# Last phase of a decoder-trunk kernel: T4 placed behind T3 and B22 for each pair, weights' parts pinned ahead of the norm's steps, three of w_out's sets stored as plain sums

## The chip, the cores and the metric

The kernel runs on one core of a Trainium2 chip. The metric is the device time of one execution in microseconds (us). Of the kernel before there are three timed runs and one profiled execution. TensorE is PE in the profile, VectorE DVE, ScalarE ACT, GpSimd POOL; SP is the engine whose queue issues most DMAs.

## The reference

One layer of a decoder trunk over 2048 positions of width 1024: adaLN modulation, a wide input projection, sliding-window attention and a pooled branch side by side, both projected and gated into y, then the part that this change is about:

```python
y = jax.nn.sigmoid(m_a) * a + jax.nn.sigmoid(m_p) * p
y = (y @ w_out[l]) * (1.0 + gate[:, None, :])
x = layer_norm(DEEPNORM_ALPHA * x + y, ln_gain[l], ln_bias[l])
```

All in float32. `layer_norm` works per position, over the 1024 columns.

## The kernel before, in words

**Products.** Every large matrix product is made of quads. A quad takes two blocks of 128 output rows and two column halves of 512, and computes its four results with seven half-size products instead of eight (Strassen-Winograd). The seven are named after the moving operand, a "set": B11, T1, T2, B21, T3, B22, T4. A set is 128x4x2x512 floats in SBUF: 4 slabs, each as a high part (the value rounded to fp32r) and a low part (the rest). The quad's own side, the "weights" W (here rows of y), is split in the same way just before use: ACT casts the high part (`CAST w_set<-W`), DVE subtracts to get the low part (`TENSOR_TENSOR w_set<-W,w_set`). A product is 12 matmuls of 128x512, three for each slab: high by high, high by low, low by high. So its first two matmuls need the cast alone.

A quad's split happens four times: **first** parts (for B11 and T1), **second** (T2, B21), **third** (T3, B22) and the half for T4. Between them POOL changes W in place: `sum1` (L294), `mid` (L298 and L299, of which L298 overwrites what the first parts are made from), `late` (L303).

**Groups and phases.** The last stage ("mix") has five phases; the fifth multiplies y by w_out. Each phase has groups of two quads, called x0 and x1 here. `ring` runs over the groups: `back` does T2 and B21 of x0 and of x1, then T3 and B22 of x0 and of x1, then T4 of x0 and of x1; `front` then opens the next group with B11 and T1 of each quad. After every product comes a `tick`, at which functions from `hooks` (set by group and position) and from the deferred list `due` are issued. In the last phase x0 holds rows 4g and 4g+1 of 128 positions, and x1 rows 4g+2 and 4g+3, for group g of 0 to 3.

**Norm.** `out_quad.consume` adds ALPHA times x to a result (L637, `wide<-wide,mm` or `wide<-wide,lg`). When both halves of a row are there, `norm_row` defers its steps by ticks: 1 sums (ACT over 128x1024), 2 mean and down (DVE, tiny) and squares (ACT), 3 rs (DVE, tiny), the power (POOL, 128x1) and (z-mean)*gain (DVE, 128x1024), 4 scale (DVE, 128x1024), 6 the store. Rows 13 to 15 use `last_norm` with BN_STATS on DVE and write the result in two halves.

**What sets the order.** Instructions issued through `act`, `dve`, `pool`, `sp` and `pe` (class `Ordered`) keep the program's order among themselves; those issued through `nc.scalar`, `nc.vector` and so on may be placed elsewhere by the scheduler that builds the program. Each engine then runs its instructions strictly as they stand. The splits by `pair_split` use `nc.scalar` and `nc.vector`, the norm's steps mostly the pinned ones.

**Sets of w_out.** They are made in the second phase of the kernel (stage "g1") by `sums_to`, split there by `kept_parts` (ACT cast, DVE low part, two stores) into `wo_d`, and loaded ready-made by `fill_set`, 1 MB a half set, by `PLAN`. Sets of other phases of "mix" are stored as plain sums, loaded as 512 KB a half into one of two `spare` tiles and split in place at `SPLIT_AT`. `planned` puts entries under 14 into the last group of the phase before, the others into the first group of the phase itself.

Of the kernel before, what the change touches and what calls it, by code (L numbers as in the profile page):

```python
# [19 lines left out]
P = 128  # L20
# [39 lines left out]
def kernel(  # L60
# [52 lines left out]
    def split_store(name):  # L113
        return {n: dp.tile([4, P, 2, CH], F32, name=f"{name}_{n}_split") for n in set_names}
# [3 lines left out]
    wo_d = split_store("wo")  # L118
# [157 lines left out]
    class Quad:  # L276
# [4 lines left out]
        def __init__(self, srcs, consume):  # L281
            self.srcs, self.consume = srcs, consume
# [69 lines left out]
    def front(ph, q, tick):  # L352
        w = pair_split(ph, q.first())
        q.mid()
        a, b = bank(), bank()
        product(a, w[0], "B11", True)
        tick()
        product(b, w[1], "T1", True)
        tick()
        return a, b, None, None  # L360

    def back(ph, grp, opened, nxt, own, tick, b22_first=False):
# [51 lines left out]
        if b22_first:  # L414
# [20 lines left out]
    def defer(ticks, f):  # L435
        due.append((now[0] + ticks, len(due), f))

    def run_due(every=False):
        while due and (every or any(d[0] <= now[0] for d in due)):
            d = min(due, key=lambda d: d[:2])  # L440
            due.remove(d)
            d[2]()

    def ring(ph, groups, opened, hooks, nxt, after, b22_first=False):
# [3 lines left out]
        def tick():  # L448
# [6 lines left out]
            run_due()  # L455

        for gi, grp in enumerate(groups):
            pos[:] = [gi, 0]
            own = gi % 2 == 0 and gi + 1 < len(groups)
            back(ph, grp, opened, (groups + [nxt])[gi + 1], own, tick, b22_first and gi == 0)  # L460
            if gi + 1 < len(groups):
                opened = [front(ph, q, tick) for q in groups[gi + 1]]
# [22 lines left out]
    def set_steps(ph, store):  # L485


        if store["B11"].shape[0] == 4:
            return [(p, lambda n=n, h=h: fill_set(n, h, store[n])) for p, n, h in PLAN]
        raw, todo = {}, []  # L490

        def fetch(k):
            name, half = PLAN[k][1:]
            raw[k] = ph.spare()
            sp.dma_start(raw[k], store[name][half].rearrange("p a b -> p (a b)"))

        def split(k):
            name, half = PLAN[k][1:]
            split_set(name, 2 * half, by_two(raw[k]), 2, (act, dve))

        for k, at in enumerate(SPLIT_AT):
            if k < 2:
                todo.append((0, lambda k=k: fetch(k)))
            todo.append((at, lambda k=k: split(k)))
            if k + 2 < len(SPLIT_AT):
                todo.append((at, lambda k=k: fetch(k + 2)))
# [78 lines left out]
    def norm_row(ph, row, z):  # L585
# [27 lines left out]
        for at, f in ((1, sums), (2, squares), (3, power), (4, scale), (6, store)):  # L613
            defer(at, f)

    def last_stats(row, n, zn):
        nc.vector.bn_stats(carry[:, row - 12, 6 * n : 6 * n + 6], zn)

    def last_norm(row, z):

        st, mv, rs = (carry[:, row - 12, a:b] for a, b in ((0, 12), (12, 14), (14, 15)))
        nc.vector.bn_aggr(mv, st)
        nc.vector.tensor_scalar(rs, mv[:, 1:2], EPS, None, ALU.add)
        nc.gpsimd.tensor_tensor(rs, rs, mhalf, ALU.pow)
        nc.vector.scalar_tensor_tensor(z, z, mv[:, 0:1], vec["gain"], ALU.subtract, ALU.mult)
        for n, q in enumerate((nc.sync, nc.scalar)):
            zn = cols(z, n)
            nc.vector.scalar_tensor_tensor(zn, zn, rs, cols(vec["lnb"], n), ALU.mult, ALU.add)  # L628
            q.dma_start(out[row * P : (row + 1) * P, n * CH : (n + 1) * CH], zn)

    def out_quad(k):
        def consume(ph, mi, n, src):
# [4 lines left out]
            nc.vector.scalar_tensor_tensor(zn, zn, ALPHA, src, ALU.mult, ALU.add)  # L637
            if row > 12:
                last_stats(row, n, zn)
            if n_done:  # L640
                if row > 12:
# [4 lines left out]
        return Quad(tuple(y_d[k + i].rearrange("p k q -> p (k q)") for i in range(2)), consume)  # L646
# [746 lines left out]
    with Pools("mix", spare=2, p=2, c=5) as ph:  # L1393
# [9 lines left out]
        for i, (groups, store) in enumerate(phases):  # L1403
# [7 lines left out]
            if i + 1 < len(phases):  # L1411
                planned(hooks, ph, phases[i + 1][1], True)
                nxt = phases[i + 1][0][0]
                after = lambda tick, nxt=nxt: [front(ph, q, tick) for q in nxt]
            else:
                for at, row in ((1, 2), (1, 3), (5, 4), (5, 5)):
# [66 lines left out]
```

## Time and profile before

| what | us |
|---|---|
| median of 3 timed runs | 1765.89 (1764.87 to 1765.94) |
| the profiled execution, its own time | 1766.12 |
| its span, first to last instruction | 1764.3 |
| PE busy in the span | 1702.9 |
| DVE, ACT, POOL busy | 1206.0, 931.8, 792.7 |
| mean granted TensorE clock | 0.992 |

The last phase begins at about 1593 us with the fronts of its first group (issued in the phase before), and its last matmul ends at about 1750. A timeline row reads: start, length (us), engine, line, operation, output<-input, shape, count, and in brackets the idle time of the engine just before and what ended it. A product of 12 matmuls takes 2.72 us from start to start. On PE `lg` and `mm` are accumulators; which product it is follows from the order T2, B21 (twice), T3, B22 (twice), T4 (twice, one row x24), then B11, T1 (twice).

### The profile page before, as it was taken

The numbers are of one execution on the slowest core, as the hardware profiler recorded it, in microseconds if no ns is written. First come the engines' busy times: TensorE is split into PE (matmuls) and PEld (weight loads), VectorE is DVE, ScalarE is ACT, GpSimd is POOL, SyncE is SP. The second block draws the span as 40 slices with busy tenths as digits, with TensorE's granted clock in tenths as the row PEclk, the third lists the DMA queues.
The fourth block names the chain that finished last, engine by engine and source line by source line (L and its number), as shares of the span: only waits on it lengthen the run. The fifth ranks groups of instructions, "written<-read, shape, count | busy, mean of one in ns | idle before, by whom it ended". The sixth has DMA issues, their size and how long they took to land. (4 is left out here: it accounts for less than half of the span.)

```text
span 1764.3 us, 24983 instructions
## 1 busy us (share of the span) xinstructions
PE 1702.9 (97%) x8248; PEld 1428.7 (81%) x8248; DVE 1206.0 (68%) x2180; ACT 931.8 (53%) x1969; POOL 792.7 (45%) x618
## 2 busy tenths in 40 slices
PE   6899999999999998999999999999999989999996
PEld 5688888888888887888788888888888768888785
DVE  5967665655777786766655367777867586765777
ACT  4544444545777775454444377777744333423451
POOL 2145454431356567434434125456762562364542
PEclk9999999999999999999999999999999999999998
DMA  9384767743354567687777634544796585689432
GB/s 365 112 279 179 270 210 273 271 148 132 108 173 146 172 219 294 245 281 254 246 274 262 231 98 132 175 155 149 258 356 225 182 257 182 226 314 384 166 143 99
DMA packets 180609, 381.30 MB, mean 216 GB/s; under 512 B 18800, under 2 KB 39296, under 8 KB 180480
## 3 DMA queue, kind: packets, MB, share of 16 engines
q1 hardware_dynamic: 173696, 363.66, 59.2%
q0 software_dynamic: 3552, 11.56, 1.7%
q10 hardware_dynamic: 3232, 4.49, 0.9%
q8 instruction: 65, 1.06, 0.2%
q14 instruction: 64, 0.52, 0.1%
HBM read 244.35 MB, written 138.44 MB: 217 GB/s over the span
## 5 line engine op out<-in xcount | busy, mean ns | idle before, releaser
L56 PE MATMUL mm<-set_B,w_set 128*128 128x512 f32 x3240 | 801.8, 396 | 17.5 <-DVE w_set L132 8.7
L56 PEld LDWEIGHTS mm<-set_B,w_set 128*128 128x128 f32 x3240 | 604.2, 189 | 147.4 <-DVE w_set L132 15.2
L56 PE MATMUL lg<-set_T,w_set 128*128 128x512 f32 x2088 | 505.9, 392 | 14.0 <-DVE w_set L132 8.6
L56 PEld LDWEIGHTS lg<-set_T,w_set 128*128 128x128 f32 x2088 | 390.8, 188 | 103.7 <-DVE w_set L132 14.0
L132 DVE TENSOR_TENSOR w_set<-W,w_set 128x1024 fp32r<-128x1024 f32 x162 | 224.1, 1383 | 175.7 <-ACT w_set L325 171.4
L325 ACT CAST w_set<-W 128x1024 fp32r<-128x1024 f32 x162 | 169.7, 1049 | 242.4 <-PE mm L56 195.6
L56 PE MATMUL mm<-set_T,w_set 128*128 128x512 f32 x1080 | 266.2, 394 | 0.0
L56 PEld LDWEIGHTS mm<-set_T,w_set 128*128 128x128 f32 x1080 | 201.1, 189 | 41.3
L294 POOL TENSOR_TENSOR W<-W,A 128x512 f32<-128x512 f32 x56 | 82.1, 1466 | 221.7 <-DMA W<-in_win_dram 55.9
L303 POOL TENSOR_TENSOR W<-W 128x512 f32<-128x512 f32 x56 | 80.1, 1431 | 155.5 <-DVE w_set L132 143.9
L56 DVE TENSOR_TENSOR o<-pv,o 64x128 f32<-64x128 f32 x256 | 72.4, 283 | 88.3 <-ACT o L56 85.4
L56 ACT ACTIVATE L<-L,nm 128x257 f32<-128x257 f32 (+1 forms) x256 | 127.2, 498 | 9.3 <-DVE nm L56 3.9
L298 POOL TENSOR_TENSOR W<-W 128x512 f32<-128x512 f32 x56 | 88.1, 1574 | 93.8 <-DVE w_set L132 84.7
L56 DVE CUSTOM_DVE_ANT_0 L<-lg,bt,nsink 128x256 f32<-128x256 f32 (+1 forms) x256 | 111.6, 473 | 5.0 <-PE lg L56 0.8
L299 POOL TENSOR_TENSOR W<-W 128x512 f32<-128x512 f32 x56 | 88.1, 1573 | 37.3 <-DMA W<-in_win_dram 28.1
L56 POOL TENSOR_TENSOR w_set<-W,w_set 128x1024 fp32r<-128x1024 f32 x14 | 33.7, 2405 | 139.6 <-ACT w_set L56 97.0
L56 POOL TENSOR_TENSOR p<-nxt,pg 128x512 f32<-128x512 f32 x32 | 42.0, 1311 | 106.4 <-DVE sm L56 102.8
L56 ACT COPY o<-pv 64x256 f32<-64x256 f32 x128 | 47.3, 370 | 78.1 <-PE pv L56 77.3
L56 DVE TENSOR_TENSOR ptl<-pt,pth 128x512 fp32r<-128x512 f32 (+1 forms) x128 | 85.7, 669 | 1.9 <-ACT pth L56 1.7
L56 DVE TENSOR_TENSOR k_lo<-spare,k_hi 128x512 fp32r<-128x512 f32 x61 | 63.2, 1041 | 28.8 <-ACT k_hi L56 15.0
L56 PE MATMUL lg<-kk,qs 128*128 128x256 f32 (+1 forms) x512 | 80.5, 279 | 0.0
L56 ACT ACTIVATE L<-L,sm 128x256 f32<-128x256 f32 (+1 forms) x128 | 64.3, 502 | 29.4 <-DVE sm L56 29.4
(208 smaller groups left out, 2304.9 us busy)
## 6 DMA issues: line engine op xcount, KB each, us to landing
W<-in_win_dram SPq DMA_DIRECT2D x48, 512.0 KB, 5.3
w_set<-wmix_d SPq DMA_DIRECT2D x32, 512.0 KB, 5.2
W<-in_win_dram SPq DMA_DIRECT2D x34, 256.0 KB, 3.4
A<-in_win_dram SPq DMA_DIRECT2D x34, 256.0 KB, 5.0
ag_d<-sig SPq DMA_DIRECT2D x32, 256.0 KB, 3.3
pg_d<-sig SPq DMA_DIRECT2D x32, 256.0 KB, 3.7
ma_d<-sig SPq DMA_DIRECT2D x32, 256.0 KB, 3.9
mp_d<-sig SPq DMA_DIRECT2D x32, 256.0 KB, 3.8
```

Of the source, the lines that this page charges most:

```text
L56: return lambda *args, **kw: self.tc.keep_in_program_order(op(*args, **kw))
L132: engine.tensor_tensor(dst, src, as32(hi), ALU.subtract)
L294: e.tensor_tensor(self.w[:, 1, :], self.w[:, 2, :], self.a22, ALU.add)
L298: e.tensor_tensor(x[:, 1, :], x[:, 1, :], x[:, 0, :], ALU.subtract)
L299: e.tensor_tensor(x[:, 2, :], x[:, 0, :], x[:, 2, :], ALU.subtract)
L303: e.tensor_tensor(x[:, 3, :], x[:, 3, :], x[:, 1, :], ALU.subtract)
L325: a.copy(by_two(hi), raw)
```

## The change

It has six parts.

1. `wo_d` keeps T3, B22 and T4 as plain sums (2x128x2x512) instead of split parts. `sums_to` stores each of them straight from the work buffer (`put`), with no cast and no subtraction; `set_steps` now decides for each set: split ones are filled as before, plain ones are fetched into a `spare` and split in place by ACT and DVE.
2. `out_quad` makes its quads `pinned`. In `back`, both T4 halves are split first; ahead of T4 of x1 the first parts of the next group's x0 are split through the pinned engines (`pinned_parts`), and in `front` those of x1 behind x0's B11.
3. The norm's steps are `soft`: the ticks behind T4 of x0 and behind x0's B11 leave them out, and `pinned_parts` issues those that are due behind its split.
4. The last group of the last phase runs pair by pair (`finish_rows`): T3, B22, T4 of x0, then B22, T3, T4 of x1.
5. Row 12 uses `last_norm` too; of rows 12 to 14 the final scale and stores are deferred by two ticks; these steps are pinned.
6. Rows 4 and 5 of x are loaded at position 9 of the first group, not 5.

```diff
-    wo_d = split_store("wo")
+    wo_d = {**split_store("wo", ("B11", "T1", "T2", "B21", "B12")), **{n: dp.tile([2, P, 2, CH], F32, name=f"wo_{n}") for n in ("T3", "B22", "T4")}}
...
-            if b12 or name != "B12":
+            if store[name].shape[0] == 2:
+                todo.append((at, lambda name=name, z=z: put(sp, store, name, i, x(*z))))
+            elif b12 or name != "B12":
...
-    def front(ph, q, tick):
-        w = pair_split(ph, q.first())
+    def front(ph, q, tick, ahead=None, follows=None):
+
+        w = ahead or pair_split(ph, q.first())
         q.mid()
         a, b = bank(), bank()
         product(a, w[0], "B11", True)
-        tick()
+        tick(not follows)
+        parts = pinned_parts(ph, follows)
         product(b, w[1], "T1", True)
         tick()
-        return a, b, None, None
+        return (a, b, None, None), parts
+
+    def pinned_parts(ph, q):
+        if q is None:
+            return None
+        w = pair_split(ph, q.first(), act, dve)
+        run_due()
+        return w
...
+        finish_rows = grp[0].pinned and not nxt
+        if finish_rows:
+            for x, (q, b, c, p5) in enumerate(st):
+                third(x)
+                w4 = half_split(ph, q.a22)
+                for f in (with_b22, with_t3) if x else (with_t3, with_b22):
+                    f(x)
+                product(c, w4, "T4")
+                tick()
+                q.consume(ph, 1, 0, c)
...
-        for q, b, c, p5 in st:
-            w = half_split(ph, q.a22)
+        ws = []
+        ahead = None
+        for x, (q, b, c, p5) in enumerate(st):
+            if q.pinned:
+                ws = ws or [half_split(ph, z[0].a22) for z in st]
+                w = ws[x]
+                if x:
+                    ahead = pinned_parts(ph, nxt[0])
+            else:
+                w = half_split(ph, q.a22)
             product(c, w, "T4")
-            tick()
+            tick(not q.pinned or x > 0)
             q.consume(ph, 1, 0, c)
+        return ahead
...
-    def run_due(every=False):
-        while due and (every or any(d[0] <= now[0] for d in due)):
-            d = min(due, key=lambda d: d[:2])
+    def run_due(every=False, soft=True):
+        while ready := [d for d in due if every or d[0] <= now[0] and (soft or not d[3])]:
+            d = min(ready, key=lambda d: d[:2])
...
+        for at, (kept_at, name, half) in zip(SPLIT_AT, PLAN):
+            if store[name].shape[0] == 4:
+                todo.append((kept_at, lambda n=name, h=half: fill_set(n, h, store[n])))
+                continue
+            todo.append((at, lambda n=name, h=half: split(n, h)))
+            fetch_at = ahead[-2] if len(ahead) > 1 else max(at - 4, 0)
+            todo.append((fetch_at, lambda n=name, h=half: fetch(n, h)))
+            ahead.append(at)
...
-            defer(at, f)
+            defer(at, f, True)
...
+        def scale():
+            for n, q in enumerate((sp, act)):
+                zn = cols(z, n)
+                dve.scalar_tensor_tensor(zn, zn, rs, cols(vec["lnb"], n), ALU.mult, ALU.add)
+                q.dma_start(out[row * P : (row + 1) * P, n * CH : (n + 1) * CH], zn)
+
+        if row < 15:
+            defer(2, scale)
+        else:
+            scale()
```

**Place 1, the passage from group 1 to group 2 of the last phase.** On DVE before (the tile after `wide` names a row: 15557 is row 4, 15771 row 6, 15559 row 5, 15825 row 7; `mean` marks (z-mean)*gain, `rs` in a `wide` row the scale, `lg` the result of T4; W_15844 belongs to x0 of the next group, W_15888 to x1):

```order
L56 SCALAR_TENSOR_TENSOR wide6_15557<-wide6_15557,mean_15867,wide0_15274 128x1024
L132 TENSOR_TENSOR w_set_15968<-W_15844,w_set_15967 128x1024
L637 SCALAR_TENSOR_TENSOR wide7_15559<-wide7_15559,lg_15751 128x512
L56 SCALAR_TENSOR_TENSOR wide6_15557<-wide6_15557,rs_15869,wide1_15276 128x1024
L56 TENSOR_SCALAR mean_15913<-total_15912 128x1
L56 TENSOR_SCALAR down_15914<-total_15912 128x1
L637 SCALAR_TENSOR_TENSOR wide3_15825<-wide3_15825,lg_15790 128x512
L132 TENSOR_TENSOR w_set_16017<-W_15888,w_set_16016 128x1024
```

On DVE now, at the same place (15610 is row 4, 15612 row 5, 15783 row 7; W_15802 is x0's, W_15846 x1's):

```order
L680 SCALAR_TENSOR_TENSOR wide7_15612<-wide7_15612,lg_15709 128x512
L56 TENSOR_TENSOR w_set_15899<-W_15802,w_set_15898 128x1024
L56 TENSOR_SCALAR rs_15827<-rs_15827 128x1
L56 SCALAR_TENSOR_TENSOR wide6_15610<-wide6_15610,mean_15825,wide0_15214 128x1024
L680 SCALAR_TENSOR_TENSOR wide3_15783<-wide3_15783,lg_15748 128x512
L56 SCALAR_TENSOR_TENSOR wide6_15610<-wide6_15610,rs_15827,wide1_15216 128x1024
L56 TENSOR_SCALAR mean_15871<-total_15870 128x1
L56 TENSOR_SCALAR down_15872<-total_15870 128x1
L56 TENSOR_TENSOR w_set_15946<-W_15846,w_set_15945 128x1024
```

The first parts of x0 moved ahead of row 4's step, but behind the result of x0's T4. On ACT before, at the same place (`total` marks sums, `down` squares):

```order
L56 ACTIVATE spare_15909,rs_15869<-wide6_15557,down_15868 128x1024
L325 CAST w_set_15967<-W_15844 128x1024
L56 ACTIVATE wide2_15771,total_15912<-wide2_15771 128x1024
L325 CAST w_set_16016<-W_15888 128x1024
L56 ACTIVATE spare_15959,rs_15915<-wide2_15771,down_15914 128x1024
L56 ACTIVATE wide7_15559,total_15937<-wide7_15559 128x1024
```

On ACT now:

```order
L56 ACTIVATE spare_15867,rs_15827<-wide6_15610,down_15826 128x1024
L56 CAST w_set_15898<-W_15802 128x1024
L56 ACTIVATE wide2_15729,total_15870<-wide2_15729 128x1024
L56 ACTIVATE spare_15921,rs_15873<-wide2_15729,down_15872 128x1024
L56 ACTIVATE wide7_15612,total_15894<-wide7_15612 128x1024
L56 CAST w_set_15945<-W_15846 128x1024
```

The cast of x1's first parts moved behind the squares of row 6 and the sums of row 5. The passages from group 0 to 1 and from 2 to 3 have the new order too.

**Place 2, the start of the last phase.** On DVE now (spare_15263 and spare_15290 hold the two halves of set T3; gp is a gate's tile of the phase before, multiplied into its result; W_15191 is x0's, W_15241 x1's):

```order
L56 TENSOR_TENSOR set_T3_13110<-spare_15263,set_T3_13110 128x2x512
L132 TENSOR_TENSOR w_set_15358<-W_15241,w_set_15357 128x1024
L605 TENSOR_TENSOR gp_15270<-mm_15068,gp_15270 128x512
L132 TENSOR_TENSOR w_set_15399<-W_15191,w_set_15398 128x1024
L56 TENSOR_TENSOR set_T3_13110<-spare_15290,set_T3_13110 128x2x512
L605 TENSOR_TENSOR gp_15294<-lg_15095,gp_15294 128x512
L132 TENSOR_TENSOR w_set_15446<-W_15241,w_set_15445 128x1024
L605 TENSOR_TENSOR gp_15315<-lg_15135,gp_15315 128x512
```

Before, the rows of set_T3 were not there, and each of the two `gp<-lg` stood one place earlier among the other six. On SP now, a little later (wo_B22 and wo_T4 are the plain sums):

```order
L56 DMA spare_15354<-wo_B22_96 128x1024
L56 DMA y_d_142<-wide5_14626 128x4x128
L56 DMA spare_15379<-wo_B22_96 128x1024
L56 DMA y_d_142<-wide7_14672 128x4x128
L290 DMA A22_15497<-y_d_142 128x512
L290 DMA A22_15539<-y_d_142 128x512
L56 DMA spare_15417<-wo_T4_97 128x1024
L289 DMA W_15496<-y_d_142 128x512
L56 DMA spare_15434<-wo_T4_97 128x1024
```

Four half sets of 512 KB stand where four of 1 MB were filled, and both A22 tiles of the next group now come ahead of T4's halves; before, they came behind them.

**Place 3, the end.** On DVE now, from the first half of row 15 on (16390 is row 15, 16337 row 14, 16111 row 13):

```order
L56 SCALAR_TENSOR_TENSOR wide_16390<-wide_16390,p_16356 128x512
L56 TENSOR_SCALAR carry<-carry 128x1
L56 SCALAR_TENSOR_TENSOR wide_16337<-wide_16337,carry,wide_15214 128x1024
L56 SCALAR_TENSOR_TENSOR wide_16111<-wide_16111,carry,wide_15216 128x512 x2
L56 BN_STATS carry<-wide_16390 128x6
L56 SCALAR_TENSOR_TENSOR wide_16337<-wide_16337,carry,wide_15216 128x512 x2
L56 SCALAR_TENSOR_TENSOR wide_16390<-wide_16390,lg 128x512
L56 BN_STATS carry<-wide_16390 128x6
```

Ahead of the last product's result (`lg`) stand the gain step of row 14 and the scales of rows 13 and 14; before, row 12's and row 13's steps stood there, and row 12 was stored last, in one piece of 512 KB.

More of the change, by code (lines that the diff above doesn't have):

```diff
@@ L459, in ring @@
             own = gi % 2 == 0 and gi + 1 < len(groups)
-            back(ph, grp, opened, (groups + [nxt])[gi + 1], own, tick, b22_first and gi == 0)
+            ahead = back(ph, grp, opened, (groups + [nxt])[gi + 1], own, tick, b22_first and gi == 0)
             if gi + 1 < len(groups):
-                opened = [front(ph, q, tick) for q in groups[gi + 1]]
+                pair = groups[gi + 1]
+                opened = []
+                for n, q in enumerate(pair):
+                    follows = pair[n + 1] if q.pinned and n + 1 < len(pair) else None
+                    o, ahead = front(ph, q, tick, ahead, follows)
+                    opened.append(o)
         result = after(tick) if after else None
@@ L485, in set_steps, with fetch, split @@
     def set_steps(ph, store):
-        if store["B11"].shape[0] == 4:
-            return [(p, lambda n=n, h=h: fill_set(n, h, store[n])) for p, n, h in PLAN]
         raw, todo = {}, []
[L492 to L506, printed above, removed]
+        def fetch(name, half):
+            raw[name, half] = ph.spare()
+            sp.dma_start(raw[name, half], store[name][half].rearrange("p a b -> p (a b)"))
+        def split(name, half):
+            split_set(name, 2 * half, by_two(raw[name, half]), 2, (act, dve))
+        ahead = []
+        for at, (kept_at, name, half) in zip(SPLIT_AT, PLAN):
[6 more added lines that the diff above has]
+            ahead.append(at)
         return todo
@@ L613, in norm_row @@
         for at, f in ((1, sums), (2, squares), (3, power), (4, scale), (6, store)):
[L614 removed]
+            defer(at, f, True)
     def last_stats(row, n, zn):
[L617 removed]
+        dve.bn_stats(carry[:, row - 12, 6 * n : 6 * n + 6], zn)
     def last_norm(row, z):
         st, mv, rs = (carry[:, row - 12, a:b] for a, b in ((0, 12), (12, 14), (14, 15)))
[L622 to L629, printed above, removed]
+        dve.bn_aggr(mv, st)
+        dve.tensor_scalar(rs, mv[:, 1:2], EPS, None, ALU.add)
+        pool.tensor_tensor(rs, rs, mhalf, ALU.pow)
+        dve.scalar_tensor_tensor(z, z, mv[:, 0:1], vec["gain"], ALU.subtract, ALU.mult)
+        def scale():
[7 more added lines that the diff above has]
+            scale()
     def out_quad(k):
```

32 lines of the change are left out of this document (17 added, 15 removed).

## The prediction

> **What bounds the kernel now.** The page first: PE is busy for nearly all of the span, at an almost full clock.
>
> ```profile
> span 1764.3 us, 24983 instructions
> PE 1702.9 (97%) x8248; PEld 1428.7 (81%) x8248; DVE 1206.0 (68%) x2180; ACT 931.8 (53%) x1969; POOL 792.7 (45%) x618
> PEclk9999999999999999999999999999999999999998
> ```
>
> So time is lost or won where PE waits. The timeline of PE in the last phase shows two such places, both in the passage from group 0 to group 1, where the fronts' first parts come late:
>
> ```profile
> 1631.13 0.61 PE L56 MATMUL mm<-set_B,w_set 128*128 128x512 f32 x2
> 1633.78 2.60 PE L56 MATMUL mm<-set_B,w_set 128*128 128x512 f32 x10 [2.03 <-DVE rs L56]
> 1639.05 0.73 PE L56 MATMUL mm<-set_B,w_set 128*128 128x512 f32 x2
> 1641.57 2.56 PE L56 MATMUL mm<-set_B,w_set 128*128 128x512 f32 x10 [1.78 <-DVE w_set L132]
> ...
> 1652.28 2.88 PE L56 MATMUL lg<-set_T,w_set 128*128 128x512 f32 x12
> ...
> 1668.60 5.60 PE L56 MATMUL lg<-set_T,w_set 128*128 128x512 f32 x24
> 1674.04 2.88 PE L56 MATMUL mm<-set_B,w_set 128*128 128x512 f32 x12
> 1679.48 2.88 PE L56 MATMUL mm<-set_B,w_set 128*128 128x512 f32 x12
> ...
> 1690.36 2.88 PE L56 MATMUL lg<-set_T,w_set 128*128 128x512 f32 x12
> ```
>
> From the end of T4 (B11 of x0 begins, 1631.13) to T2 of x1 (1652.28) are 21.15 us; the same stretch of the next passage, 1674.04 to 1690.36, takes 16.32 with no gap in it. So the passage 0 to 1 costs **4.8 us** and the passages 1 to 2 and 2 to 3 cost nothing. The chain that ended last says why the first is late, a transfer:
>
> ```profile
> 1613.37 13.77 DMA A<-y_d
> 1627.30 1.22 POOL W L294
> ```
>
> The A tile took 13.77 us to land, and sum1 (L294), the cast and the subtraction came after it. The third place is the end: the last matmul ends at 1744.76 + 5.60 = 1750.36, the span at 1764.3.
>
> **The change, part by part.** *Passages between groups.* This decides. I follow the new order through the passage 1 to 2 with the durations of before, from these rows of DVE, POOL and ACT:
>
> ```profile
> 1671.80 0.69 DVE L637 SCALAR_TENSOR_TENSOR wide<-wide,lg 128x512 f32<-128x512 f32 x1
> 1674.98 1.21 DVE L132 TENSOR_TENSOR w_set<-W,w_set 128x1024 fp32r<-128x1024 f32 x1
> 1676.18 1.27 DVE L56 SCALAR_TENSOR_TENSOR wide<-wide,mean,wide 128x1024 f32<-128x1024 f32 x1
> 1679.14 1.28 DVE L56 SCALAR_TENSOR_TENSOR wide<-wide,rs,wide 128x1024 f32<-128x1024 f32 x1 [1.56 <-POOL rs L56]
> 1682.13 1.29 DVE L56 SCALAR_TENSOR_TENSOR wide<-wide,rs,wide 128x1024 f32<-128x1024 f32 x1 [0.32 <-POOL rs L56]
> 1687.50 1.29 DVE L56 SCALAR_TENSOR_TENSOR wide<-wide,rs,wide 128x1024 f32<-128x1024 f32 x1 [1.70 <-POOL rs L56]
> 1688.70 1.22 DVE L132 TENSOR_TENSOR w_set<-W,w_set 128x1024 fp32r<-128x1024 f32 x1
> ...
> 1671.97 1.29 POOL L298 TENSOR_TENSOR W<-W 128x512 f32<-128x512 f32 x1 [0.81 <-DVE w_set L132]
> 1676.28 2.33 POOL L298 TENSOR_TENSOR W<-W 128x512 f32<-128x512 f32 x1 [3.02 <-DVE rs L56]
> 1678.56 0.55 POOL L56 TENSOR_TENSOR rs<-rs,mhalf 128x1 f32<-128x1 f32 x1
> ...
> 1669.81 1.05 ACT L56 ACTIVATE wide<-wide 128x1024 f32<-128x1024 f32 x1
> 1671.57 1.06 ACT L325 CAST w_set<-W 128x1024 fp32r<-128x1024 f32 x1 [0.61 <-POOL rs L56]
> 1674.56 1.15 ACT L56 ACTIVATE spare<-wide,down 128x1024 f32<-128x1024 f32 x1 [1.94 <-DVE down L56]
> ```
>
> From start to start a 1024-wide step takes DVE 1.2 us (1.28 with overlap), a split 1.14, a result's 512 columns 0.6. Before, x1's first parts were cast at 1671.57 and subtracted by 1676.1, over 3 us ahead of B11 of x1 (1679.48). Now: T4 of x0 ends at 1668.60 + 2.72 = 1671.32. DVE takes its result first (until 1671.95), then splits x0 (1673.1, in time for 1674.04). Behind that come row 4's gain step (1674.35) and, on POOL, mid (L298) and only then row 4's power. Mid started at 1676.28, 0.1 us behind such a gain step (1676.18), and took 2.33 us for what took 1.29 at 1671.97; so it ends near 1675.5 and the power (0.55) near 1676.1. Then the scale (1677.3) and row 6's mean and down (1677.45); on ACT row 6's squares (1.15), row 5's sums (1.14) and now at last the cast of x1 (1.0) until 1680.8; the subtraction until 1681.95. B11 of x1 can start its first two matmuls early (0.45 us of work), so it needs them by 1679.93: PE waits **2.0**. From there to x1's second parts DVE does what it did before from 1676.12 (the end of the row at 1674.98, by the pitch) to 1688.70, 12.6 us, plus T2's addition 0.6 and the split 1.14: 14.3 us, to 1696.25. T2 of x1 would want them at 1690.36 + 2.0 + 0.45: **3.4** more. Before, the slack of 3.8 us at B11 of x1 covered this; now the stretch starts when PE is already waiting. Of the 12.6 us, 3.6 are waits for POOL (1.56, 0.32 and 1.70 in the rows above), and two gain steps now stand together, so a little may be packed. Bounds for a passage: if mid ran beside the gain step the first wait would be 0.9, and without those 3.6 us of waits the second would be 0; so 0.9 below, and above 6.5, with one more blocked operation of 1.1 on each engine's way. I take **5.0**, near what the rows give. All three passages have this order, also the first, whose late transfer goes (A now stands ahead of T4's halves, and 3 MB are not loaded). 3 x 5.0 - 4.8 = **+10.2**.
>
> The rule of the Trainium skill, SBUF — State Buffer, section "SBUF: two separate sides", speaks against this order: VectorE operations with two SBUF inputs and GpSimd's share a port pair, and whoever starts first holds it for the whole instruction. The trace agrees: L298 took 2.33 us behind a gain step. Were there no such lock, each first wait would be 1.1 us shorter, and the sum 3.3 lower.
>
> *Start of the phase.* T3, B22 and T4 come as half sets of 512 KB, split in place. The DMA engines are full there:
>
> ```profile
> 1596.00:1600.00 4.00, 4.00 (x19) 3.33 (x18) 1.93 (x2) 1.89 (x3) 2.84 (x3) 1.00 1.04 400
> 1600.52 0.69 DVE L569 TENSOR_TENSOR gp<-lg,gp 128x512 f32<-128x512 f32 x1 [2.20 <-DMA gp<-mp_d]
> 1601.24 0.57 ACT L368 COPY lg<-mm 128x512 f32<-128x512 f32 x1 [1.24 <-DVE gp L569]
> 1603.93 2.88 PE L56 MATMUL lg<-set_T,w_set 128*128 128x512 f32 x12
> 1505.76 1.22 DVE set_T L56
> ```
>
> At 400 GB/s 512 KB take 1.3 us. Both halves of T3 are now fetched ahead of the gp tile for which DVE waited at 1600.52, so it lands 2.6 later, at 1603.1. The second T3 half's subtraction (1.22, as that of the plain set at 1505.76) stands ahead of it on DVE and ends near 1604.0; gp's product follows to 1604.6 and ACT's copy of the accumulator (0.57) to 1605.2. T2 of x0 wanted it at 1603.93: **+1.3**, between 0 (the fetch runs in a gap) and 2.6 (both transfers on the way). The six casts (1.06) and subtractions (1.22) lie beside matmuls otherwise; without that cover they would be 7.3 us on DVE.
>
> *Stage g1.* Twelve fewer casts and twelve fewer subtractions:
>
> ```profile
> L56 DVE TENSOR_TENSOR k_lo<-spare,k_hi 128x512 fp32r<-128x512 f32 x56 | 56.9, 1021 | 28.8 <-ACT k_hi L56 15.0 <-DMA ag_d<-sig 3.0 <-DMA wo_B_split<-k_lo 2.6
> L56 ACT CAST k_hi<-spare 128x512 fp32r<-128x512 f32 x56 | 34.5, 617 | 35.7 <-POOL spare L56 8.1 <-DMA ma_d<-sig 7.1 <-DMA pg_d<-sig 3.3
> 850.56 0.73 PE L56 MATMUL lg<-set_T,w_set 128*128 128x512 f32 x2 [1.11 <-ACT w_set L325]
> 869.91 5.30 PE L56 MATMUL lg<-set_T,w_set 128*128 128x512 f32 x22 [1.47 <-DVE w_set L132]
> ```
>
> That is 12 x 1.02 and 12 x 0.62 us of engines that PE waits for here, 2.6 us in the two rows (1.11 and 1.47). Those waits lie at casts that stay. The new stores read the work buffer, and POOL's next sum and the next fetch wait for them; SP is in order, so the W loads behind could wait as well. From -2.6 (both waits go) to +2.0 (a load queued behind a store); I take **-0.5**, as most waits keep their cause.
>
> *The end.* Rows of DVE and SP:
>
> ```profile
> 1744.76 5.60 PE L56 MATMUL lg<-set_T,w_set 128*128 128x512 f32 x24
> 1753.98 0.68 DVE L637 SCALAR_TENSOR_TENSOR wide<-wide,lg 128x512 f32<-128x512 f32 x1
> 1758.66 1.42 DVE L628 SCALAR_TENSOR_TENSOR wide<-wide,carry,wide 128x512 f32<-128x512 f32 x2 [0.44 <-POOL carry L624]
> 1759.82 0.42 SPq L56 DMA_DIRECT2D out_dram<-wide  x1
> ```
>
> Before, DVE reached the last result 3.6 us after PE's end (1753.98), since row 13's steps came ahead; the last scale began 4.7 later. Now row 13 is done earlier, but row 14's gain step, both of its scales and row 13's scales stand ahead of it. From B22 of x0 on the order has three gain steps (1.2), three pairs of scales (1.4), ten operations of 0.6, a split (1.14) and 0.6 of small ones, 15.5 us for PE's four products of 2.72, 10.9: DVE reaches the last result at about +5, the scales end near +10.0, where they ended at 1760.1 - 1750.4 = +9.7. What goes is row 12's 512 KB store behind it all (1759.82): the last halves land without it. **-0.7**, between -2.5 (DVE catches up) and +1.0. Rows 4 and 5 of x, loaded four ticks later, are first used six products (16 us) behind, more than the 13.77 that A took: nothing.
>
> Sum: 10.2 + 1.3 - 0.5 - 0.7 = +10.3 on the profiled execution's 1766.12, so 1776.4; the median lies 0.2 lower, at 1765.89, which gives **1776.2 us**.
>
> **Rivals.** (1) *It does what its order suggests*: the late A tile goes, x0's parts come in time, and x1's are not held up, because sums and squares are ahead of need. Then 4.8 go, and 0.7 at the end: 1760.4. For it: the chain's 13.77 us transfer. Against: the cast of x1 stands behind squares that need DVE's scale. (2) *Only the first wait comes*: DVE's waits for POOL are packed away, 3 x 2.0 - 4.8 + 1.3 - 0.5 - 0.7 = +1.3, so 1767.2. For it: 3.6 us of waits in that stretch; against: the power still stands behind mid and late on POOL. (3) *The plain sums become the bound*: T4's fetch waits for B22's split, SP is in order behind it, and row 2 and the next W are late; DVE then holds the T4 halves of the weights. If these transfers take the 10 us or more that A took, PE waits 5 to 6 more: 1782. It decides if a half set takes over 8 us to land; the queue is shorter by 3 MB, which speaks against it.
>
> **How the numbers follow.** My forecast (the passages wait, 1769.5 to 1780) has 0.69, rival 1 0.14, rival 2 0.11, rival 3 0.06. A measurement of this kernel can tell about 0.2%, 3.5 us, from no change: faster 0.14, same 0.11, slower 0.75. With passages of 0.9 to 6.5 the forecast's sum reaches from rival 2 to 1781; leaving out rival 1 and rival 3's far part gives 1764 to 1781.
>
> **What would show it.** In the changed kernel's PE timeline: a gap ahead of B11 of x1 of 1.5 to 2.5 us, released by DVE's first parts, and one of 2 to 4 ahead of T2 of x1, in all three passages, with x0's B11 on time; a wait of about 1 us at the first T2 of the phase; DVE at the last result some 5 us after PE. Wrong if passages 1 to 2 and 2 to 3 stay without gaps, or if the gaps stand at T3 or T4 instead (rival 3).

## The result and the profile after

The changed kernel takes **1775.95 us** (median of 5 runs, 1774.86 to 1777.4), the kernel before 1765.81 beside it (5 runs, 1763.29 to 1765.94). The ratio is 1.0059, with a 95% interval of 1.0047 to 1.007: the change costs about 10 us. Its profiled execution took 1775.31 us, 9.2 more than that of before (1766.12). The page of the changed kernel:

```profile
span 1773.4 us, 24914 instructions
PE 1706.4 (96%) x8248; PEld 1430.0 (81%) x8248; DVE 1201.0 (68%) x2176; ACT 927.1 (52%) x1959; POOL 786.4 (44%) x618
PEclk9999999999999999999999999999999999999999
```

DVE, ACT and POOL have each become less busy than before (1206.0, 931.8 and 792.7), and the matmuls are the same 8248. PE's busy time grew by 3.5 us for the same work: some matmuls took longer. The rest is waiting. PE's timeline in the passages between groups of the last phase (start, length, engine, line, operation, count, and in brackets the idle time ahead and what ended it):

```profile
1627.37 0.73 PE L56 MATMUL mm<-set_B,w_set 128*128 128x512 f32 x2
1628.62 2.58 PE L56 MATMUL mm<-set_B,w_set 128*128 128x512 f32 x10 [0.52 <-DVE w_set L56]
...
1636.32 4.75 PE L56 MATMUL mm<-set_B,w_set 128*128 128x512 f32 x12 [2.40 <-ACT w_set L56]
1640.91 2.90 PE L56 MATMUL mm<-set_T,w_set 128*128 128x512 f32 x12
...
1651.22 2.60 PE L56 MATMUL lg<-set_T,w_set 128*128 128x512 f32 x10 [1.52 <-DVE w_set L132]
1653.66 2.89 PE L56 MATMUL mm<-set_B,w_set 128*128 128x512 f32 x12
...
1672.70 2.88 PE L56 MATMUL mm<-set_B,w_set 128*128 128x512 f32 x12
1675.42 2.88 PE L56 MATMUL mm<-set_T,w_set 128*128 128x512 f32 x12
1679.73 0.73 PE L56 MATMUL mm<-set_B,w_set 128*128 128x512 f32 x2 [1.43 <-ACT w_set L56]
1680.99 2.57 PE L56 MATMUL mm<-set_B,w_set 128*128 128x512 f32 x10 [0.53 <-DVE rs L56]
1683.40 2.88 PE L56 MATMUL mm<-set_T,w_set 128*128 128x512 f32 x12
...
1694.64 3.92 PE L56 MATMUL lg<-set_T,w_set 128*128 128x512 f32 x10 [2.40 <-DVE w_set L132]
1698.40 2.88 PE L56 MATMUL mm<-set_B,w_set 128*128 128x512 f32 x12
...
1717.44 2.88 PE L56 MATMUL mm<-set_B,w_set 128*128 128x512 f32 x12
...
1739.37 2.56 PE L56 MATMUL lg<-set_T,w_set 128*128 128x512 f32 x10 [2.40 <-DVE w_set L132]
1741.77 2.88 PE L56 MATMUL mm<-set_B,w_set 128*128 128x512 f32 x12
```

Seven products lie between B11 of x0 and B21 of x1, 7 x 2.72 = 19.04 us without a gap. In the passage 1 to 2 it is 1698.40 - 1672.70 = 25.70, so 6.7 us are lost; in 2 to 3, 1741.77 - 1717.44 = 24.33, 5.3 lost; in 0 to 1, from 1627.31 (the end of T4, as its matmuls are spaced) to 1653.66, 7.3 lost. That is 19.3 in three passages, where before lost 4.8 in one. Both waits stand where the order puts x1's parts: one at its B11 and one at its T2. What DVE, ACT and POOL do in the passage 1 to 2:

```profile
1670.79 1.22 DVE L56 TENSOR_TENSOR w_set<-W,w_set 128x1024 fp32r<-128x1024 f32 x1
1671.99 1.27 DVE L56 SCALAR_TENSOR_TENSOR wide<-wide,mean,wide 128x1024 f32<-128x1024 f32 x1
1674.96 1.29 DVE L56 SCALAR_TENSOR_TENSOR wide<-wide,rs,wide 128x1024 f32<-128x1024 f32 x1 [1.09 <-POOL rs L56]
1679.71 1.23 DVE L56 TENSOR_TENSOR w_set<-W,w_set 128x1024 fp32r<-128x1024 f32 x1 [3.35 <-ACT w_set L56]
1690.37 2.48 DVE L56 SCALAR_TENSOR_TENSOR wide<-wide,rs,wide 128x1024 f32<-128x1024 f32 x2 [0.44 <-POOL rs L56]
1693.37 1.22 DVE L132 TENSOR_TENSOR w_set<-W,w_set 128x1024 fp32r<-128x1024 f32 x1
...
1676.46 1.15 ACT L56 ACTIVATE spare<-wide,down 128x1024 f32<-128x1024 f32 x1 [6.85 <-DVE down L56]
1678.65 1.03 ACT L56 CAST w_set<-W 128x1024 fp32r<-128x1024 f32 x1
...
1672.09 2.33 POOL L300 TENSOR_TENSOR W<-W 128x512 f32<-128x512 f32 x1 [6.70 <-DVE rs L56]
1674.38 0.55 POOL L56 TENSOR_TENSOR rs<-rs,mhalf 128x1 f32<-128x1 f32 x1
```

This is the chain of the prediction, link by link: x0's subtraction (1670.79), row 4's gain step (1671.99), beside it POOL's `mid` (L300 in this kernel) for 2.33 us and only then the power (1674.38), the scale (1674.96), row 6's squares on ACT (1676.46), and behind these the cast of x1 (1678.65), for which DVE waits 3.35 us. Then the rows' steps run on until the two scales at 1690.37 end, and x1's second parts (1693.37) come behind them.

To see the other terms, the start times of matmul number n are compared in both traces; a stretch's difference is how much longer it took than before. Until 845 us +0.5, in g1 from there on (where PE's waits of before stand) -2.7, from g1 to the last phase -1.7, the start of the last phase +0.45, the passages +14.4, and the last group with what follows PE's end -1.55: +9.3 from the first matmul on, which began 0.3 us earlier.

### The profile page after: what moved, and what is told of

The parts are those of the page before. It is cut to its first block, busy times and chain, and to the rows that moved or that the text cites. A ratio compares the mean times of both kernels' runs of the same rounds, so it can differ in the third digit from the quotient of the medians.

```text
span 1773.4 us, 24914 instructions
## 1 busy us (share of the span) xinstructions
PE 1706.4 (96%) x8248; PEld 1430.0 (81%) x8248; DVE 1201.0 (68%) x2176; ACT 927.1 (52%) x1959; POOL 786.4 (44%) x618
## 5 line engine op out<-in xcount | busy, mean ns | idle before, releaser
L132 DVE TENSOR_TENSOR w_set<-W,w_set 128x1024 fp32r<-128x1024 f32 x156 | 217.7, 1396 | 186.2 <-ACT w_set L327 179.3
L327 ACT CAST w_set<-W 128x1024 fp32r<-128x1024 f32 x156 | 163.7, 1050 | 239.9 <-PE mm L56 193.1
L300 POOL TENSOR_TENSOR W<-W 128x512 f32<-128x512 f32 x56 | 90.6, 1619 | 127.6 <-DVE w_set L132 90.8
L56 ACT CAST pth<-pt 128x512 fp32r<-128x512 f32 (+1 forms) x128 | 73.4, 573 | 10.2
```

The lines of the kernel that those rows point to most:

```text
L56: return lambda *args, **kw: self.tc.keep_in_program_order(op(*args, **kw))
L132: engine.tensor_tensor(dst, src, as32(hi), ALU.subtract)
L300: e.tensor_tensor(x[:, 1, :], x[:, 1, :], x[:, 0, :], ALU.subtract)
L327: a.copy(by_two(hi), raw)
```

## The experiments

The theory: the pinned order makes x1's parts late, by two waits in each passage. Rivals: the plain sums with their transfers, or the pair-by-pair end, cost the time. Each verdict below goes by the ratio to the kernel before, run on the same chip. The table has in us, against before: g1 from 845 us on; the start of the last phase; the three passages; the end (the last group and what follows PE's last matmul).

| kernel | median, us | ratio, 95% interval | g1 | start | passages | end |
|---|---|---|---|---|---|---|
| changed | 1775.95 | 1.0059 (1.0047 to 1.007) | -2.7 | +0.45 | +14.4 | -1.55 |
| e1_unpinned | 1762.18 | 0.9968 (0.9957 to 0.998) | -2.4 | 0.0 | -2.1 | -1.55 |
| e2_pin_only | 1785.47 | 1.0096 (1.0081 to 1.0111) | -1.0 | 0.0 | +17.7 | -0.1 |
| e3_sums_only | 1764.53 | 0.998 (0.997 to 0.9991) | -2.2 | +2.9 | -3.8 | +0.5 |
| e4_both_ahead | 1777.36 | 1.0052 (1.0035 to 1.0069) | -3.0 | 0.0 | +10.1 | -1.6 |
| e5_power_first | 1783.71 | 1.0089 (1.0074 to 1.0104) | -3.9 | +1.9 | +17.3 | -1.55 |
| e6_t3_first | 1777.67 | 1.0058 (1.0043 to 1.0073) | -2.2 | +1.1 | +14.7 | -1.0 |
| e9_steps_early | 1773.75 | 1.0033 (1.0022 to 1.0044) | -2.2 | +0.6 | +9.5 | -1.6 |
| e10_both_early | 1761.72 | 0.9965 (0.9949 to 0.9981) | -3.9 | +2.2 | -3.5 | -1.5 |
| e11_no_sums | 1761.01 | 0.997 (0.9958 to 0.9982) | -0.8 | 0.0 | -3.05 | -1.3 |
| e12_both_early_again | 1760.39 | 0.9968 (0.9956 to 0.9981) | -3.0 | +0.1 | -1.1 | -1.6 |

Each row of the last four columns is one execution. e10 and e12 are the same kernel, and their starts differ by 2.1 us and their passages by 2.4, so a single number of this table is no better than that; what stands alike in many rows is.

**Three parts apart.** e1 is the changed kernel without its pinning, e2 and e3 are the kernel before with one part added.

```diff
 e1, from the changed kernel
-            self.srcs, self.consume, self.pinned = srcs, consume, pinned
+            self.srcs, self.consume, self.pinned, self.by_pair = srcs, consume, False, pinned
...
-        finish_rows = grp[0].pinned and not nxt
+        finish_rows = grp[0].by_pair and not nxt
```

> The changed kernel without the pinning: the last phase's accumulators are updated by plain sums as before, the parts of the next group's weights stand where the order of work put them before, the last group still runs pair by pair and three of w_out's sets stay plain sums. Theory (the pinned order makes the second quad's parts late: about 14 us of PE's waits in the three passages between groups): these waits fall back to the 4.8 us that they were before, the shorter waits ahead of the last phase stay, and the time is about 1760 to 1763 us. Rival (the plain sums of w_out with their transfers, or the pair-by-pair end, cost the time): it stays at about 1773 to 1777 us.

```diff
 e2, from the changed kernel; last_norm and last_stats also as before
-    wo_d = {**split_store("wo", ("B11", "T1", "T2", "B21", "B12")), **{n: dp.tile([2, P, 2, CH], F32, name=f"wo_{n}") for n in ("T3", "B22", "T4")}}
+    wo_d = split_store("wo")
...
-        finish_rows = grp[0].pinned and not nxt
+        finish_rows = False
...
-                for at, row in ((1, 2), (1, 3), (9, 4), (9, 5)):
+                for at, row in ((1, 2), (1, 3), (5, 4), (5, 5)):
```

> The kernel before with the pinning alone: the weights' parts stand ahead of the norm's steps in the last phase, without plain sums and without the pair-by-pair end. Theory: the passages between groups wait about 14 to 19 us as in the changed kernel, and neither the gain ahead of the last phase nor that of the end is there, so the time is about 1776 to 1781 us. Rival (the plain sums or the end cost the time): about 1766 us, as the kernel before.

```diff
 e3, from the kernel before; set_steps as in the change
-    wo_d = split_store("wo")
+    wo_d = {**split_store("wo", ("B11", "T1", "T2", "B21", "B12")), **{n: dp.tile([2, P, 2, CH], F32, name=f"wo_{n}") for n in ("T3", "B22", "T4")}}
...
-            if b12 or name != "B12":
+            if store[name].shape[0] == 2:
+                todo.append((at, lambda name=name, z=z: put(sp, store, name, i, x(*z))))
+            elif b12 or name != "B12":
```

> The kernel before with the plain sums alone: T3, B22 and T4 of w_out are not split before the last phase. Theory: the waits ahead of the last phase shrink by about 2.5 us in that stretch and those of two phases earlier by up to 1.8 us, and the first passages stay as they were, so the time is 1761 to 1764 us. Rival (the additional transfers of the last phase collide with its loads): 1768 to 1776 us.

Without the pinning the passages lose nothing over before and the kernel is 0.32% faster than before (1762.18 us); with the pinning alone it is 0.96% slower, the worst of all. Its passages lose 17.7 us more than those of before, 22.5 in all, and so lie above what the theory gave, as its time does: 3.0 of the 3.3 us that it loses more than the changed kernel are in the passage 0 to 1 (10.3 against 7.3). The plain sums alone are 0.2% faster, by half a microsecond outside the theory's range. So the pinned order is the price, and both rivals fall: what they blame is a small gain.

The traces also show where the plain sums help behind g1. Of the A tiles issued from 1600 to 1645 us, the slowest landed 12.6 to 14.1 us after its issue in the three kernels without them (before, e2 and e11), and at most 5.4 us after it in the nine executions with them. That is the late transfer of the kernel before, and in e3 the passage 0 to 1 loses 1.0 us instead of 4.8.

**Which part of the pinned order.** Two things make x1's parts late: its cast is issued behind row 6's squares, and the norm's steps begin later, since row 4's gain is held back until x0's parts are split. e4 undoes the first, e9 the second, e10 both, all with the pinning kept.

```diff
 e4, from the changed kernel
-            tick(not q.pinned or x > 0)
+            tick(not q.pinned)
             q.consume(ph, 1, 0, c)
-        return ahead
+        if ahead:
+            return [ahead, pinned_parts(ph, nxt[1])]
...
-                    follows = pair[n + 1] if q.pinned and n + 1 < len(pair) else None
-                    o, ahead = front(ph, q, tick, ahead, follows)
-                    opened.append(o)
+                    opened.append(front(ph, q, tick, ahead and ahead[n])[0])
```

> The changed kernel with the first parts of the second quad's weights (B11's cast and difference) put ahead of the norm's steps too, so that they stand behind no square and no gain. Theory: the wait of about 2 us at the second quad's B11 goes from the three passages, the one at its T2 stays or grows by up to 2 us (the norm's steps begin later), and the time is about 1768 to 1773 us. Rival (the waits come from the additional vector work of the pinned order in sum, not from the place of the cast): it stays at 1774 to 1778 us. A third way (both waits hang on that one cast): 1762 to 1766 us.

```diff
 e9, from the changed kernel
-        tick(not follows)
+        tick()
...
-            tick(not q.pinned or x > 0)
+            tick()
```

> The changed kernel with the pinning kept, but with the norm's steps no longer held back at the first quad's T4 and B11: row 4's gain stands ahead of the first quad's difference again, and so on. The second quad's first cast now stands behind two or three more of the steps on ACT and DVE. Theory (the two waits of a passage are two ends of one queue: what is put ahead in DVE's order takes its time from the other): the second wait (at the second quad's T2, about 2.4 us) falls under 1 us, and the first (at its B11) grows from about 2 to 4 to 6 us, so the time is 1772 to 1780 us. Rival (holding the steps back is the whole price): both waits fall, to 1763 to 1768 us.

```diff
 e10, from e4
-            tick(not q.pinned)
+            tick(not q.pinned or x == 0)
```

> The kernel with both quads' first parts ahead (as in the run above that put the second quad's parts ahead too), but with row 4's gain ahead of the first quad's difference again, so that the chain of the norm's steps begins about 1.3 to 3 us earlier. Theory (after that run the only wait left in a passage is the 3.2 us at the second quad's T2, and it is the length of the norm's chain from its late start): that wait falls to 0.5 to 2 us, B11 waits at most 1 us more, and the time is 1766 to 1772 us. Rival (the chain's start is not what it hangs on): 1775 to 1778 us.

PE in the passage 1 to 2 of e4, its B11 of x0 and of x1, and T2 of x1 but for its first two matmuls:

```profile
1675.80 2.88 PE L56 MATMUL mm<-set_B,w_set 128*128 128x512 f32 x12
...
1681.24 2.88 PE L56 MATMUL mm<-set_B,w_set 128*128 128x512 f32 x12
...
1696.05 4.01 PE L56 MATMUL lg<-set_T,w_set 128*128 128x512 f32 x10 [3.22 <-DVE w_set L132]
```

The same passage of e9; these are all its gaps:

```profile
1680.62 0.73 PE L56 MATMUL mm<-set_B,w_set 128*128 128x512 f32 x2 [1.25 <-ACT w_set L56]
1681.88 3.78 PE L56 MATMUL mm<-set_B,w_set 128*128 128x512 f32 x10 [0.53 <-DVE w_set L56]
```

And of e10, B11 and T2 of x1:

```profile
1676.63 2.88 PE L56 MATMUL mm<-set_B,w_set 128*128 128x512 f32 x12
...
1687.51 2.88 PE L56 MATMUL lg<-set_T,w_set 128*128 128x512 f32 x12
```

e4 has only the second wait, e9 only the first, e10 neither (but for a rest in the passage 0 to 1): with early cast and early steps the kernel takes 1761.72 us, 0.35% below before, and below the range that the theory gave. Each wait has a cause of its own, though they aren't quite independent: without the first, PE was at T2 earlier, and the second grew from 2.40 to 3.22 us. Both theories of e9 are corrected too: the idle time of the first wait did not grow (1.25 us against 1.43), so it isn't the other end of one queue, and holding back the steps isn't the whole price either. Its cost did grow, as slow matmuls followed it: T2 of x0 came 4.0 us late there (1688.66), 2.5 in the changed kernel. In e4 the passages cost 4.3 us less than in the changed kernel, but its time can't be told from that kernel's, and lies in the range of its rival; the rest of that execution was slower. What exactly the early steps cure was not taken apart further: in e9 and e10 the chain begins earlier, and the scheduler also puts x1's second subtraction ahead of row 7's scale.

**POOL's part in the chain.** e5 keeps `mid` behind the power.

```diff
 e5, from the changed kernel
-        q.mid()
+        q.mid(pool if q.pinned and ahead else nc.gpsimd)
```

> The changed kernel with POOL's two differences for T1 and T2 (of the weights of the first parts) kept behind a row's power on POOL, instead of ahead of it. Theory (the chain of the norm's steps sets when the second quad's parts are ready, and each of these differences with its 2.33 us stands in that chain): the waits of DVE for POOL's power (1.09 and 1.57 us in a passage) fall to about 0.4 us each, the two waits of PE in a passage shrink by 1 to 2 us together, and the time is 1769 to 1773 us. Rival (the chain has slack there, or the differences now come too late for T1 and T2): 1774 to 1780 us.

DVE's scale of row 4 and POOL's power and `mid` in the passage 1 to 2 of e5:

```profile
1682.01 2.22 DVE L56 SCALAR_TENSOR_TENSOR wide<-wide,rs,wide 128x1024 f32<-128x1024 f32 x1
...
1680.38 1.52 POOL L56 TENSOR_TENSOR rs<-rs,mhalf 128x1 f32<-128x1 f32 x1 [9.18 <-DVE rs L56]
1681.87 3.51 POOL L56 TENSOR_TENSOR W<-W 128x512 f32<-128x512 f32 x2
```

The wait of DVE for the power (1.09 us) went, but the scale itself now takes 2.22 us instead of 1.29, and the power 1.52 instead of 0.55: x1's first parts come 8.68 us behind x0's (1679.02 to 1687.70), where they came 8.92 behind them in the changed kernel. And x1's `mid`, kept behind one row's power, now stands ahead of another's:

```profile
1697.04 3.52 POOL L56 TENSOR_TENSOR W<-W 128x512 f32<-128x512 f32 x2
...
1701.10 1.28 DVE L56 SCALAR_TENSOR_TENSOR wide<-wide,rs,wide 128x1024 f32<-128x1024 f32 x1 [1.69 <-POOL rs L56]
```

In the changed kernel the last two scales ran together at 1690.37. Here the last waits 1.69 us for its power, and x1's second parts (1702.90) come 15.20 us behind its first instead of 13.66. The passages grew by 2.9 us and the kernel is slower, by more than the rival gave. The part of the theory that says `mid` can simply be moved out of the chain falls: beside a DVE step one of the two is late, and behind one power it is in the way of the next. The Trainium skill, SBUF — State Buffer, section "SBUF: two separate sides", has the rule for the first of these, that the engine that starts first holds the shared ports for the whole instruction. The rows agree: POOL's `mid` took 2.33 us behind DVE's step in the changed kernel, and DVE's scale 2.22 behind `mid` here.

**The end.** T4 of x1 waits in the changed kernel because it adds onto the bank that DVE's addition behind T3 (L416) must read first. e6 puts B22 between the two.

```diff
 e6, from the changed kernel
-                for f in (with_b22, with_t3) if x else (with_t3, with_b22):
+                for f in (with_t3, with_b22):
```

> The changed kernel with T3 ahead of B22 for the second pair of the last group as well. Theory (T4 of that pair waits 2.16 us because DVE reads T3's bank late, behind the last rows' steps): with one more product between T3 and T4 this wait falls under 0.5 us; DVE's own queue at the end then sets the last result, so the time falls by 0 to 2 us, to 1774 to 1776 us. Rival (T4 waits for something else): the wait stays at about 2 us and the time at 1776 us.

DVE and PE at the end of the changed kernel:

```profile
1757.79 1.28 DVE L56 SCALAR_TENSOR_TENSOR wide<-wide,carry,wide 128x1024 f32<-128x1024 f32 x1
1758.98 0.69 DVE L56 BATCH_NORM_STATS2 carry<-wide 128x6 f32<-128x512 f32 x1
1759.59 0.68 DVE L416 TENSOR_TENSOR p<-lg,p 128x512 f32<-128x512 f32 x1
1760.41 3.00 PE L56 MATMUL lg<-set_T,w_set 128*128 128x512 f32 x12 [2.16 <-DVE carry L56]
1765.41 0.68 DVE L56 SCALAR_TENSOR_TENSOR wide<-wide,lg 128x512 f32<-128x512 f32 x1
1768.88 1.41 DVE L56 SCALAR_TENSOR_TENSOR wide<-wide,carry,wide 128x512 f32<-128x512 f32 x2 [0.44 <-POOL carry L56]
```

And of e6:

```profile
1762.70 2.91 PE L56 MATMUL lg<-set_T,w_set 128*128 128x512 f32 x12
1769.19 0.68 DVE L56 SCALAR_TENSOR_TENSOR wide<-wide,lg 128x512 f32<-128x512 f32 x1
1772.66 2.74 DVE L56 SCALAR_TENSOR_TENSOR wide<-wide,carry,wide 128x512 f32<-128x512 f32 x4 [0.44 <-POOL carry L56]
```

The wait went, as the theory said, and the time did not fall (1.0058). DVE sets the end: the last result came 2.0 us behind PE's end in the changed kernel (1765.41 against 1763.41), 3.6 in e6 (1769.19 against 1765.61), and four scales stand at its end instead of two. The table says the same: in e4, e9, e10 and the changed kernel T4 took between 3.00 and 4.58 us, and the end was worth -1.5 to -1.6 in all of them. That wait is cover for DVE, not a price.

**The plain sums in place.** e11 is e10 with all eight sets of w_out split ahead (`wo_d = split_store("wo")`), e12 is e10 again, both on one chip.

> The best kernel so far (both quads' first parts ahead, row 4's gain ahead of the first quad's difference) without the plain sums: all eight sets of w_out are split before the last phase, as in the kernel before. Theory (the plain sums gain about 2 us ahead of the last phase, where T3, B22 and T4 are no longer split, and give 0 to 3 us back at the start of the last phase): the waits ahead of the last phase grow by 1 to 2.5 us, the wait at the start of the last phase (1.8 us at T2 in the run before) goes, and the time stays within 2 us of the kernel with the plain sums, 1760 to 1764 us. Rival 1 (the sums are a clear gain): 1764 to 1767 us. Rival 2 (they are a clear loss): 1756 to 1759 us.

> The same kernel as the run with both quads' first parts ahead and row 4's gain early, again, on the same chip as the one without plain sums: 1760 to 1764 us by the theory that its passages between groups wait for nothing; the other theories of that run expected 1766 us and more.

PE's longest wait in g1 from 845 us on, first of e11, then of e12:

```profile
869.57 5.32 PE L56 MATMUL lg<-set_T,w_set 128*128 128x512 f32 x22 [1.47 <-DVE w_set L132]
```

```profile
867.66 5.32 PE L56 MATMUL lg<-set_T,w_set 128*128 128x512 f32 x22 [0.64 <-DVE w_set L132]
```

By the table the sums are worth 2.2 us more in g1 (-3.0 against -0.8) and the start varies between 0.0 and 2.9 us with them, where it is 0.0 without them. The times, 1760.39 and 1761.01 us, can't be told apart, as the theory expected. Both runs of this kernel beat the kernel before and the changed one: 0.9968 / 1.0059 = 0.991 of the latter's time.

## Why the prediction held, and where its sizes were off

The forecast of 1776.2 us (10.3 us slower on the profiled execution) met 1775.95 (9.2 slower there). The mechanism of the main term was right; that the sum came within 0.3 us of the time is luck, as the terms show:

- **The passages, +10.2 predicted, +14.4 measured.** Right in place and cause, and e1 shows that the pinned order is what it hangs on. The first wait was put at 2.0 us, and cost 2.5 to 2.6 in each passage (T1 of x1 would have followed at 1680.86 without a gap and came at 1683.40). The second was put at 3.4, and cost 1.8 to 2.8 without the slower matmuls below; in the passage 2 to 3 both make 5.3, where 5.0 was predicted. The term was too small for two things that it left out: matmuls at half the clock behind a wait, 1.87 us at 1636.32 (4.59 from B11 to T1 instead of 2.72) and 1.36 at 1694.64 (3.92 instead of 2.56), and x0's B11 in the first passage, 0.95 us late. The prediction had x0's parts in time in all three. A part of the 1.87 came back: PE reached the second wait of that passage later, and it was 0.9 shorter there (1.8 against 2.8).
- **The cause within the passage.** The prediction followed one chain, in which the second wait stands on the first. e4 and e9 show two: each can be cured singly, and the other wait stays.
- **The start, +1.3 predicted, +0.45 measured.** The predicted wait, at T2 of x0 behind a late gp tile, is not in the changed kernel, which loses 0.35 of its 0.45 us at T3 of x1 (from 1616.08 to 1619.15, 0.35 over 2.72) and 0.10 at T2 of x0. It is in e10:

```profile
1600.94 2.21 DVE L56 TENSOR_TENSOR set_T<-spare,set_T 128x1024 fp32r<-128x1024 f32 x1 [1.28 <-ACT set_T L56]
1603.78 0.57 ACT L379 COPY lg<-mm 128x512 f32<-128x512 f32 x1 [2.88 <-DVE gp L604]
1604.40 3.06 PE L56 MATMUL lg<-set_T,w_set 128*128 128x512 f32 x12 [1.80 <-ACT lg L379]
```

  What is late there is T3's second half: its cast waited 1.38 us for the transfer, its subtraction for the cast, and took 2.21 us instead of 1.22, and DVE's product into gp (1603.07) follows at once. That the gp tile landed late, too, is not shown. Over the nine executions with plain sums the start costs 0.0 to 2.9 us, 1.0 on average, and 0.0 in the two without: the wait behind T3's split is there, its bounds of 0 to 2.6 were nearly right, and one execution doesn't say what it costs.
- **g1, -0.5 predicted, -2.7 measured.** The mis-sized term: "most waits keep their cause" was wrong. The waits of 1.11 and 1.47 us became one of 0.97 in the changed kernel. The two executions without sums have -0.8 and -1.0 as well, so about 0.9 of it is the profiled execution of before; the sums are worth some 2 us, near the bound of -2.6.
- **The end, -0.7 predicted, -1.55 measured.** DVE reached the last result 2.0 us behind PE, not 5: PE itself ended later, by the 2.3 us wait at T4 of x1, which the prediction didn't have. As DVE is what the end waits for, that wait cost nothing.
- **Elsewhere -1.25**, which nothing predicted (+0.5 ahead of g1 and -1.7 between g1 and the last phase). Most of it lies between 1357 and 1450 us, in the last stage, where the changed kernel gained 1.6. In the ten experiments this stretch came out between -1.85 and +1.3, with the same code there: no effect of the change is shown.

Too small by 4.2 in the passages, too large by 3.9 in the start, g1 and the end, and -1.25 elsewhere: the sum came out nearer than its terms. One statement of the forecast's range does not follow from its working: with passages of 0.9 its sum is 1763.9, not rival 2's 1767.2; the range that it gives in the end (1764 to 1781) is right. Rival 1 (the order does what it suggests) describes no run of this change, but it does describe e10, in which the passages 1 to 2 and 2 to 3 lose nothing and 0 to 1 loses 1.3.

## What to carry to other kernels

When work is pinned ahead of a chain on the same engines, ask for both what the pinned work now stands behind and what the chain, starting later, will still hold up: here each had its own wait, and curing one alone left the kernel slower than before. Pin the early split as far ahead as its data allow, but don't hold back the first link of the chain, which had slack before it. And look for the engine that sets the end before removing a wait of another: the 2.2 us at T4 were free.

## What the runs showed of the hardware

A wait of PE can cost more than its length. Two of PE's waits with an idle time of 2.40 us, and the stretch behind each (time, then busy time and instructions of PE, PEld, DVE, ACT, POOL, then the granted clock, DMA share and GB/s), in the changed kernel:

```profile
1636.30:1639.30 3.00, 2.94 (x6) 1.94 (x7) 2.61 (x5) 3.00 (x6) 1.70 (x1) 0.50 0.03 5
1694.00:1697.00 3.00, 2.36 (x6) 1.88 (x7) 3.00 (x3) 0.00 (x0) 1.28 (x1) 0.53 1.00 343
```

The granted clock was 0.50 and 0.53 for about 3 us, which made the waits dearer by 1.87 and 1.36 us; behind the third such wait, at 1739.37, ten matmuls took their usual 2.56. In e9 two idle times of 1.25 and 0.53 us with two matmuls between them were enough (1681.88, 3.78 us), while 1.43 and 0.53 were not in the changed kernel (1680.99, 2.57). The Trainium skill, TensorE: Matmul & The Clock Gate, section "What's actually happening", lets the clock fall to half after an idle window of about 3.4 us, counted by a window that runs freely. The free window agrees with the chance in these rows; that a whole window must be idle does not: 2.40 us were enough here.

Slow matmuls cost nothing, though, where PE would have waited anyway. In e6 ten matmuls behind the first wait of the passage 1 to 2 took 4.14 us (granted clock 0.72 from 1684 to 1690 us), and the second wait fell from 2.40 to 0.87, as x1's second parts came 13.65 us behind its first, no later than in the changed kernel (13.66):

```profile
1685.34 4.14 PE L56 MATMUL mm<-set_B,w_set 128*128 128x512 f32 x10 [0.53 <-DVE rs L56]
...
1698.98 2.57 PE L56 MATMUL lg<-set_T,w_set 128*128 128x512 f32 x10 [0.87 <-DVE w_set L132]
```

That passage lost 5.3 us, as much as the passage 2 to 3 of the changed kernel, in which none ran at half the clock.
